# Memory attention's transposes and value products drawn together, and a delta-rule output moved, in a two-layer decoder trunk

## The chip, the cores and the metric

The kernel runs on one core of one Trainium2 chip. The metric is the device time of one execution in microseconds (us); the time before is the median of three runs.

## The reference, cut to what matters

Two layers over 256 tokens of 1024 channels. Each has a feed-forward block, then three token mixers in parallel on one normalised stream (a gated delta rule, a sliding-window attention, an attention over 256 memory rows), a gated merge, and a second feed-forward block. The change touches the memory attention and the order in which the delta rule's outputs are made:

```
def memory_cross_attention(q, mem_n, w_mem_kv):
    ...
    s = jnp.einsum('bshd,bmhd->bhsm', q, k).astype(jnp.float32) * (XA_DH ** -0.5)
    p = jax.nn.softmax(s, axis=-1)
    o = jnp.einsum('bhsm,bmhd->bshd', p.astype(v.dtype), v)
...
    def step(S, xs):
        q_i, qk_i, u_i, w_i, kt_i, gl_i = xs
        v_new = u_i - jnp.einsum('bhcd,bhde->bhce', w_i, S)
        o = jnp.einsum('bhcd,bhde->bhce', q_i, S) + jnp.einsum('bhcs,bhse->bhce', qk_i, v_new)
...
    gates = jax.nn.sigmoid(gates.reshape(B_, S_, N_BRANCH, D))
    merged = jnp.sum(gates * jnp.einsum('bsnc,ncd->bsnd', branches, w_branch), axis=2)
```

## The kernel before, in words

Weights come in one stream of units (128 x 1024 fp32) through SyncE's DMA queue into four `raw` buffers. ScalarE casts each to `whi` and VectorE forms the rest `wlo` (both at L123, five buffers each); TensorE then computes three fp32r products per tile (`mm3`), which is what the 128x512 rows named `acc` are. Small matrices of the mixers stay in plain fp32.

TensorE's order inside `mixers` is the order of the code (`pinned`). `weave(work, steps)` runs a generator of large projections and, after its n-th piece, the small steps that `steps` lists under n. `gates(n)` has eight pieces, one weight unit with 12 products of 128x512 each; `branch(n, o)` has four. The order is gates(0), branch(0), gates(1), branch(1), gates(2), branch(2), output projection. ScalarE, VectorE and the queues each run in an order that the scheduler fixes when the program is built.

The steps that matter here, for token blocks 0 and 1 (`tb` or `c`):

- `x_scores(tb)`: scores and softmax of the memory attention, into `prs[tb]` (tile `pp`, four ScalarE multiplies at L694 end it). `x_turn(tb)` (L698): 8 transposes into two accumulator banks, copied to `pt` by ScalarE and VectorE (L704). `x_values(tb)` (L706): 8 fp32 matmuls with the values into one bank (a timeline shows two passes for each fp32 matmul, so 16), split into `oX` by a cast and a subtraction (L123).
- The delta rule: `rec_s1` gives S1 (copied at L933). `rec_r1` multiplies it, and VectorE forms R1 from it head by head (L938, four instructions). `rec_v1` needs R1 and its result is copied at L945. `rec_qs` is read by VectorE at L942. `rec_o0` makes block 0's output from matrices that are long there; it is copied at L954, and `finish(0)` squares it (L912), sums (L913), takes an inverse root in small VectorE instructions and ends in two products (L918, L919). `rec_o1` does the same for block 1 (adding at L949). `finish_turn(c)` transposes the finished block for branch(2).

Accumulator banks come from three pools: `acc` four, `at` two, `sm` two. A step that draws a bank waits until the bank's last content has been read. All `rec_` steps, the products at L663 and `finish_turn` draw from `sm`; scores, `x_turn` and `x_values` from `at`.

Of the kernel before, what the change touches and what calls it, by code (L numbers as in the profile page):

```python
# [38 lines left out]
def tile_trunk(ctx, tc, x, xT, mem, memT_, wst, lnp, memln, cvw, rows, cst, out):  # L39
# [22 lines left out]
    def T(pool, shape, tag, dt=F32, bufs=None):  # L62
        pool = pn if pool is pu and tag in NEAR else pool
        kw = {} if bufs is None else {"bufs": bufs}
        return pool.tile(shape, dt, tag=tag, name=nm(tag), **kw)
# [4 lines left out]
    def at():  # L70
        return T(psT, [P, 512], "at")

    def sm():
        return T(psS, [P, 512], "sm")
# [47 lines left out]
    def split(hi, lo, src):  # L122
        return nc.scalar.copy(hi, src).ins, nc.vector.tensor_tensor(lo, src, hi.bitcast(F32), op=ALU.subtract).ins  # L123
# [7 lines left out]
    def matmul(*a, **k):  # L131
        return pe(nc.tensor.matmul(*a, **k))  # L132

    def transpose(*a):
        return pe(nc.tensor.transpose(*a))  # L135
# [7 lines left out]
    def weave(work, steps):  # L143

        for n, _ in enumerate(work, 1):
            for f in steps.get(n, ()):
                f()
# [369 lines left out]
    def mixers(l, hT, mkT, mv_, post):  # L517
# [141 lines left out]
        def products(c, hh):  # L659
            cc = slice(c * P, (c + 1) * P)  # L660
            ps = sm().rearrange("p (h a c) -> p h a c", h=2, a=2)
            for j in range(2):
                h = 2 * hh + j  # L663
                matmul(ps[:, j, 0, :], kT[:, h, cc], kT[:, h, cc], start=True, stop=True)
                matmul(ps[:, j, 1, :], kT[:, h, cc], qT[:, h, cc], start=True, stop=True)
            for j in range(2):
                h = 2 * hh + j
                nc.vector.scalar_tensor_tensor(AK[c][:, h], TM[c][:, 1][:, h, :].unsqueeze(1).to_broadcast([P, 2, P]), cS[:, c, h:h + 1], ps[:, j], op0=ALU.mult, op1=ALU.mult)
# [9 lines left out]
        def x_scores(tb):  # L678
            ts = slice(tb * P, (tb + 1) * P)
            pr = prs[tb] = T(p2, [P, 4, S], "pp")  # L680
            mxs = T(p3, [P, 4], "mx")
            sums = T(p3, [P, 4], "sums")
            for hh in range(2):
                ps = at().rearrange("p (h k) -> p h k", h=2)
                for j in range(2):
                    h = 2 * hh + j
                    mm3(ps[:, j, :], [t[:, h, ts] for t in xq], [t[:, h, :] for t in mkT], True, True)
                nc.vector.tensor_reduce(mxs[:, 2 * hh:2 * hh + 2], ps, axis=AX.X, op=ALU.max)
                nc.vector.tensor_scalar(mxs[:, 2 * hh:2 * hh + 2], mxs[:, 2 * hh:2 * hh + 2], -xs, None, ALU.mult)
                for j in range(2):  # L690
                    h = 2 * hh + j
                    nc.scalar.activation(pr[:, h, :], ps[:, j, :], AF.Exp, bias=mxs[:, h:h + 1], scale=xs, accum_out=sums[:, h:h + 1])
            nc.vector.reciprocal(sums, sums)
            [nc.scalar.mul(pr[:, h, :], pr[:, h, :], sums[:, h:h + 1]) for h in range(4)]  # L694
# [3 lines left out]
        def x_turn(tb):  # L698
            pT = prs[2 + tb] = T(p2, [P, 2, 4, P], "pt")
            for kb in range(2):  # L700
                ps = at().rearrange("p (h k) -> p h k", h=4)
                for h in range(4):
                    transpose(ps[:, h, :], prs[tb][:, h, kb * P:(kb + 1) * P], ident)
                (nc.vector.tensor_copy if kb else nc.scalar.copy)(pT[:, kb], ps)  # L704

        def x_values(tb):  # L706
            if not oX:
                oX.extend(T(pu, [P, 4, S], tag, F32R) for tag in ("u6", "u7"))
            ts = slice(tb * P, (tb + 1) * P)
            ps = at().rearrange("p (h k) -> p h k", h=4)  # L710
            for h in range(4):
                for kb in range(2):
                    matmul(ps[:, h, :], mv_[:, kb, h * P:(h + 1) * P], prs[2 + tb][:, kb, h, :], start=kb == 0, stop=kb == 1)
            split(oX[0][:, :, ts], oX[1][:, :, ts], ps)
# [245 lines left out]
        def gates(n):  # L960
            gt = gts[n] = [T(p2, [P, D], "gt") for _ in range(2)]
            for j in range(2):
                js = slice(j * 512, (j + 1) * 512)
                outs = [acc() for _ in range(2)]
                for uu in range(KD // 2):
                    hi, lo = unit()
                    for tb in range(2):
                        ts = slice(tb * P, (tb + 1) * P)
                        for kk in range(2):
                            k, c = 2 * uu + kk, slice(kk * 512, kk * 512 + 512)  # L970
                            mm3(outs[tb], (xt[0](k)[:, ts], xt[1](k)[:, ts]), (hi[:, c], lo[:, c]), k == 0, k == KD - 1)
                    if uu < KD // 2 - 1:
                        yield
                for tb in range(2):
                    nc.scalar.activation(gt[tb][:, js], outs[tb], AF.Tanh, scale=0.5)
                yield

        def branch(n, o):
# [16 lines left out]

        weave(gates(0), {
            1: [lambda: x_scores(1), lambda: products(1, 0), lambda: products(1, 1), inverses],
            3: [lambda: x_turn(0)],
            4: [lambda: x_values(0)],
            5: [lambda: x_turn(1)],  # L1000
            6: [lambda: x_values(1)],
            7: [lambda: w_scores(0, 0)],
            8: [lambda: w_scores(0, 1)]})
        weave(branch(0, oX), {
# [14 lines left out]
            3: [rec_s1],  # L1019
            4: [rec_r1]})  # L1020
        weave(gates(2), {
            1: [rec_o0],
            2: [rec_v1, rec_qs],
            3: [rec_o1],
            5: [lambda: finish_turn(0)],
            8: [lambda: finish_turn(1)]})
# [44 lines left out]
    ps = sm()  # L1071
# [15 lines left out]
    for l in range(NL):  # L1087
        mT = []
        mid = memory_T(mT, l)
        if l == 0:  # L1090

            more = {4: lambda *a: xres(0), 6: lambda *a: xres(1), 8: lambda *a: small()}
        post = Post(lnp[l, 0, 0], lnp[l, 0, 1])
        f1.rest(hT, 4, [((pu, "u0"), (pu, "u1")), ((pu, "u2"), (pu, "u3"))], post, mid, ends, {} if l else more)
        kv = memory_kv(mT, post.end)
        if l == 0:
            nc.scalar.activation(nea, rw[:, :, 8:12], AF.Exp)
            nc.vector.tensor_scalar(nea, nea, -1.0, None, ALU.mult)
        post2 = Post(lnp[l, 1, 0], lnp[l, 1, 1])
        mixers(l, post.hT, *kv, post2)  # L1100
        f2 = Ffn()
        begin(f2, post2.hT)
        last = l == NL - 1
        post = Post(lnp[l, 2, 0], lnp[l, 2, 1], last)
        f2.rest(post2.hT, 6, [((pu, a), (pu, b)) for a, b in (("u0", "u1"), ("u2", "u3"), ("u4", "u5"), ("u6", "u13"))], post, behind=post2.end)
        ends = post.end
        if not last:
            f1, hT = Ffn(), post.hT
            begin(f1, hT)
# [87 lines left out]
```

## Time and profile before

| | |
|---|---|
| median of 3 runs | 1274.8 us (1274.46 to 1275.08) |
| profiled execution, its own time | 1274.36 us |
| its span, first to last instruction | 1272.6 us |
| TensorE busy | 1260.9 us (99%) |
| VectorE busy | 865.0 us (68%) |
| ScalarE busy | 660.8 us (52%) |
| GpSimd busy | 206.9 us (16%) |
| mean granted clock of TensorE | 0.999 |

The profiled execution took 1.8 us more than its span, which is what lies around the first and the last instruction. In timelines a row is an instruction or a run of like ones: start, duration, engine, line, operation, tiles (out<-in), shapes, count, and in brackets the idle time of the engine before it with what ended it. Consecutive matmuls overlap in these rows, so what one costs is the distance between starts and not the duration shown.

### The profile page before, as it was taken

The page shows a single profiled execution, that of the slowest core. Times are in us where ns is not written, and L with a number is a line of the kernel's source. Part 1 is how long each engine was busy: PE and PEld are TensorE (multiplying, and loading weights), DVE is VectorE, ACT ScalarE, POOL GpSimd, SP SyncE. Part 2 cuts the span into 40 slices and gives each one's busy share as a digit, 9 for nine tenths or more (in the row PEclk, how much of TensorE's full clock was granted, in tenths as well). Part 3 has the DMA queues.
Part 4 walks back from the last instruction along what each step waited for, and adds up shares of the span by engine and source line. Part 5 has one row for each costly group of instructions (what it writes and reads, how often), then busy time and mean ns, then how long its engine had stood idle before and what let it go on. Part 6 is the DMA issues. An engine that isn't in the chain of part 4 may idle for free.

```text
span 1272.6 us, 18763 instructions
## 1 busy us (share of the span) xinstructions
PE 1260.9 (99%) x6948; PEld 1073.9 (84%) x6948; DVE 865.0 (68%) x1271; ACT 660.8 (52%) x980; POOL 206.9 (16%) x365
## 2 busy tenths in 40 slices
PE   9999999999999999999999999999999999999997
PEld 6888889999878888888888888899987788888886
DVE  5788576897657776665676665759867388666555
ACT  6556444655664544544454554456556564444541
POOL 0232100002311102221012220000024101122200
PEclk9999999999999999999999999999999999999999
DMA  8988755655534748777667877556453356577772
GB/s 296 305 274 280 254 209 164 206 166 142 171 118 138 245 135 264 240 242 221 218 208 242 255 254 215 182 184 213 152 168 133 100 185 229 172 247 244 241 231 73
DMA packets 77499, 261.40 MB, mean 205 GB/s; under 512 B 11904, under 2 KB 13056, under 8 KB 77408
## 3 DMA queue, kind: packets, MB, share of 16 engines
q1 hardware_dynamic: 66320, 232.53, 56.1%
q0 software_dynamic: 11088, 27.68, 7.8%
q8 instruction: 54, 0.88, 0.3%
q14 instruction: 37, 0.30, 0.1%
HBM read 246.40 MB, written 13.76 MB: 204 GB/s over the span
## 4 chain that ended last, share of the span: by engine, by line
PE 96%; DVE 2%; DMA 1%; ACT 1%; issue 0%; SPq 0%; DVEq 0%; ACTq 0%
PE acc L132 85%; PE at L132 4%; PE sm L132 3%; PE sm L135 2%; DVE wlo L123 1%; DMA raw<-in_wst_dram 1%; PE acc L326 1%; PE acc L327 1%; PE acc L329 1%; PE at L135 1%; ACT whi L123 1%; DVE h L289 0%; DVE pp L734 0%; DVE w L938 0%; SPq L115 0%
## 5 line engine op out<-in xcount | busy, mean ns | idle before, releaser
L123 DVE TENSOR_TENSOR wlo<-raw,whi 128x1024 fp32r<-128x1024 f32 (+2 forms) x403 | 488.8, 1220 | 284.9 <-ACT whi L123 282.8
L123 ACT CAST whi<-raw 128x1024 fp32r<-128x1024 f32 (+2 forms) x403 | 413.5, 1033 | 403.7 <-PE acc L132 322.0
L132 PE MATMUL acc<-whi,hT 128*128 128x512 f32 (+1 forms) x1824 | 562.7, 386 | 0.9 <-ACT whi L123 0.9
L132 PEld LDWEIGHTS acc<-whi,hT 128*128 128x128 f32 x1824 | 340.3, 188 | 70.1 <-ACT whi L123 2.5
L132 PE MATMUL acc<-wlo,hT 128*128 128x512 f32 (+1 forms) x912 | 350.3, 384 | 0.5 <-DVE wlo L123 0.5
L132 PE MATMUL acc<-whi,u 128*128 128x512 f32 x812 | 259.6, 392 | 0.0
L132 PEld LDWEIGHTS acc<-wlo,hT 128*128 128x128 f32 x912 | 171.4, 188 | 33.5 <-DVE wlo L123 1.2
L132 PEld LDWEIGHTS acc<-whi,u 128*128 128x128 f32 x812 | 152.3, 188 | 32.1 <-DVE u L123 0.5
L132 PE MATMUL acc<-wlo,u 128*128 128x512 f32 x406 | 158.2, 390 | 0.0
L356 POOL DMA_DIRECT2D tr<-t x176 | 96.3, 554 | 304.5 <-DVE t L350 296.4
L132 PE MATMUL acc<-hT,whi 128*128 128x256 f32 x672 | 122.2, 284 | 0.0
L132 PEld LDWEIGHTS acc<-hT,whi 128*128 128x128 f32 x672 | 104.6, 192 | 0.0
L132 PE MATMUL acc<-hT,wlo 128*128 128x256 f32 x336 | 95.0, 283 | 0.0
L132 PEld LDWEIGHTS acc<-wlo,u 128*128 128x128 f32 x406 | 76.3, 188 | 15.3
L132 PEld LDWEIGHTS acc<-hT,wlo 128*128 128x128 f32 x336 | 64.3, 192 | 0.0
L357 POOL DMA_DIRECT2D pt<-tr x44 | 25.0, 569 | 200.1 <-DMA tr<-t 129.1
L347 ACT ACTIVATE t<-acc 128x256 f32<-128x256 f32 x88 | 33.5, 380 | 37.1 <-PE acc L132 37.1
L132 PE MATMUL acc<-u,u 128*128 128x512 f32 x186 | 46.4, 394 | 0.0
L348 DVE TENSOR_TENSOR t<-t,acc 128x256 f32<-128x256 f32 x88 | 36.6, 416 | 8.6 <-ACT t L347 5.3
L993 POOL TENSOR_TENSOR u<-u,gt 128x512 f32<-128x512 f32 x16 | 20.7, 1295 | 124.9 <-DVE gt L991 124.9
L132 PEld LDWEIGHTS acc<-u,u 128*128 128x128 f32 x186 | 34.6, 188 | 7.5
L546 DVE SCALAR_TENSOR_TENSOR t<-acc,cw,t 128x255 f32<-128x255 f32 (+2 forms) x72 | 34.4, 478 | 1.0
(236 smaller groups left out, 1158.3 us busy)
## 6 DMA issues: line engine op xcount, KB each, us to landing
raw<-in_wst_dram SPq DMA_DIRECT2D x409, 512.0 KB, 4.4
tr<-t POOLq DMA_DIRECT2D x176, 64.0 KB, 3.9
pt<-tr POOLq DMA_DIRECT2D x44, 256.0 KB, 4.9
raw<-in_wst_dram SPq DMA_DIRECT2D x16, 324.0 KB, 3.0
gB<-in_lnp_dram SPq DMA_DIRECT2D x6, 512.0 KB, 5.4
bB<-in_lnp_dram SPq DMA_DIRECT2D x6, 512.0 KB, 6.2
w<-dr POOLq DMA_DIRECT2D x4, 512.0 KB, 11.0
t<-in_xT_dram SPq DMA_DIRECT2D x4, 256.0 KB, 5.4
```

What stands on the lines that cost most here:

```text
L123: return nc.scalar.copy(hi, src).ins, nc.vector.tensor_tensor(lo, src, hi.bitcast(F32), op=ALU.subtract).ins
L132: return pe(nc.tensor.matmul(*a, **k))
L135: return pe(nc.tensor.transpose(*a))
L326: nc.tensor.matmul(ps, hT[0][:, k, ts], hi[:, c], start=k == 0, stop=False)
L327: nc.tensor.matmul(ps, hT[0][:, k, ts], lo[:, c], start=False, stop=False)
L329: nc.tensor.matmul(ps, hT[1][:, k, ts], hi[:, c], start=False, stop=k == KD - 1)
L347: act = nc.scalar.activation(t[:, :, tb, :], g, AF.Silu).ins
L348: ins = nc.vector.tensor_tensor(t[:, :, tb, :], t[:, :, tb, :], u, op=ALU.mult).ins
L356: nc.gpsimd.dma_start(d[:, :, q].rearrange("b c x -> c b x"), z[32 * q:32 * q + 32].rearrange("c (b x) -> c b x", b=4))
L357: back = nc.gpsimd.dma_start(y, d.rearrange("b c q x -> (b c) (q x)")).ins
L546: nc.vector.scalar_tensor_tensor(yc[:, j, d:], b[:, j, :S - d], w[:, t:t + 1], yc[:, j, d:], op0=ALU.mult, op1=ALU.add)
L993: nc.gpsimd.tensor_tensor(mg[tb][:, js], mg[tb][:, js], gt[tb][:, js], op=ALU.add)
```

## The change: three groupings per layer

In gates(0), block 0's transposes move from piece 3 to piece 4 and block 1's from piece 5 to piece 4; block 0's value products move from piece 4 to piece 6, beside block 1's. Block 1's transposes draw their banks from `sm` and no longer from `at`. In gates(2), `rec_o0` moves from piece 1 to piece 2, behind `rec_v1` and `rec_qs`. No operation is added or removed.

```diff
         def x_turn(tb):
             pT = prs[2 + tb] = T(p2, [P, 2, 4, P], "pt")
             for kb in range(2):
-                ps = at().rearrange("p (h k) -> p h k", h=4)
+                ps = (sm if tb else at)().rearrange("p (h k) -> p h k", h=4)
                 for h in range(4):
                     transpose(ps[:, h, :], prs[tb][:, h, kb * P:(kb + 1) * P], ident)
...
         weave(gates(0), {
             1: [lambda: x_scores(1), lambda: products(1, 0), lambda: products(1, 1), inverses],
-            3: [lambda: x_turn(0)],
-            4: [lambda: x_values(0)],
-            5: [lambda: x_turn(1)],
-            6: [lambda: x_values(1)],
+            4: [lambda: x_turn(0), lambda: x_turn(1)],
+            6: [lambda: x_values(0), lambda: x_values(1)],
             7: [lambda: w_scores(0, 0)],
             8: [lambda: w_scores(0, 1)]})
...
         weave(gates(2), {
-            1: [rec_o0],
-            2: [rec_v1, rec_qs],
+            2: [rec_v1, rec_qs, rec_o0],
             3: [rec_o1],
             5: [lambda: finish_turn(0)],
             8: [lambda: finish_turn(1)]})
```

TensorE in gates(0) of the first layer, before (`cs` holds the identity, `pp` the probabilities, `pt` their transposes, `u_339` the values, `acc` rows belong to the gate projection):

```order
L132 MATMUL acc_2967<-whi_3104,hT_1598 128x512
L135 MATMUL at_3122<-cs,pp_2848 128x128 x4
L135 MATMUL at_3128<-cs,pp_2848 128x128 x4
L132 MATMUL acc_2966<-whi_3135,hT_1598 128x512
...
L132 MATMUL at_3156<-pt_3121,u_339_1830 128x128 x8
...
L135 MATMUL at_3188<-cs,pp_2986 128x128 x4
L135 MATMUL at_3194<-cs,pp_2986 128x128 x4
...
L132 MATMUL at_3218<-pt_3187,u_339_1830 128x128 x8
```

The same stretch of TensorE after the change:

```order
L132 MATMUL acc_2967<-whi_3122,hT_1598 128x512
L135 MATMUL at_3142<-cs,pp_2848 128x128 x4
L135 MATMUL at_3148<-cs,pp_2848 128x128 x4
L135 MATMUL sm_3155<-cs,pp_2986 128x128 x4
L135 MATMUL sm_3161<-cs,pp_2986 128x128 x4
L132 MATMUL acc_3167<-whi_3170,hT_1598 128x512
...
L132 MATMUL at_3207<-pt_3141,u_339_1830 128x128 x8
L132 MATMUL at_3218<-pt_3154,u_339_1830 128x128 x8
```

Four groups between projection pieces became two, and the second block's transposes fill `sm` banks.

TensorE in gates(2) of the first layer, before (`sm_3963` is `rec_o0`, `sm_4008` is `rec_v1`, `sm_4015` is `rec_qs`):

```order
L132 MATMUL acc_3943<-whi_3945,hT_1598 128x512
L132 MATMUL sm_3963<-w_461_2586,u_463_2588 128x128 x4
L132 MATMUL acc_3942<-whi_3991,hT_1598 128x512
...
L132 MATMUL sm_4008<-w_462_2587,w_471_2598 128x128 x4
L132 MATMUL sm_4015<-w_462_2587,u_386_2071 128x128 x4
```

The same stretch after the change, where `sm_3980` is `rec_v1`, `sm_3987` is `rec_qs` and `sm_3994` is `rec_o0`:

```order
L132 MATMUL acc_3943<-whi_3945,hT_1598 128x512
L132 MATMUL acc_3942<-whi_3963,hT_1598 128x512
...
L132 MATMUL sm_3980<-w_462_2587,w_471_2598 128x128 x4
L132 MATMUL sm_3987<-w_462_2587,u_386_2071 128x128 x4
L132 MATMUL sm_3994<-w_461_2586,u_463_2588 128x128 x4
```

`rec_o0` no longer stands ahead of a whole projection piece and of `rec_v1`, and three steps in a row now draw from the two `sm` banks.

VectorE around R1 (L938) in gates(2) after the change:

```order
L123 TENSOR_TENSOR wlo_4117<-raw_4115,whi_4116 128x1024
L938 SCALAR_TENSOR_TENSOR w_462_2587<-sm_3931,neg_460_2585,u_390_2075 128x128 x2
L123 TENSOR_TENSOR wlo_4135<-raw_4133,whi_4134 128x1024
L942 TENSOR_TENSOR t_697_3986<-sm_3987,eg_2584 128x512
L913 TENSOR_REDUCE oms_4001<-t_701_4000 128x4
...
L949 TENSOR_TENSOR t_697_3986<-t_697_3986,sm_4039 128x512
L123 TENSOR_TENSOR wlo_4153<-raw_4151,whi_4152 128x1024
...
L913 TENSOR_REDUCE oms_4046<-t_710_4045 128x4
L919 TENSOR_TENSOR t_705_4018<-t_705_4018,u_383_2058 128x512
```

Up to the last L938 the order is that of before; behind it block 0's finishing (L913 to L919), which came right after L938, now begins behind a weight split and L942 and has L949, a second split and block 1's L913 among its instructions.

## Rows read from the trace of the kernel before

**Rows 1.** The page: busy time of each engine, clock by slices, chain that ended last.

```profile
PE 1260.9 (99%) x6948; PEld 1073.9 (84%) x6948; DVE 865.0 (68%) x1271; ACT 660.8 (52%) x980; POOL 206.9 (16%) x365
...
PEclk9999999999999999999999999999999999999999
...
PE 96%; DVE 2%; DMA 1%; ACT 1%; issue 0%; SPq 0%; DVEq 0%; ACTq 0%
```

**Rows 2.** Waits of TensorE inside the mixers: total us, times, longest.

```profile
PE at L132 <- DVE pp L734: 0.4, 2, 0.2
PE sm L132 <- DVE w L938: 0.3, 2, 0.2
```

**Rows 3.** Timeline of TensorE, gates(0), first layer.

```profile
306.53 0.39 PE L132 MATMUL acc<-whi,hT 128*128 128x512 f32 x1
306.76 1.03 PE L135 MATMUL at<-cs,pp 128*128 128x128 f32 x8
...
307.86 0.39 PE L132 MATMUL acc<-wlo,hT 128*128 128x512 f32 x1
...
310.15 0.40 PE L132 MATMUL acc<-whi,hT 128*128 128x512 f32 x1
310.39 1.95 PE L132 MATMUL at<-pt,u 128*128 128x128 f32 x16
...
312.40 0.40 PE L132 MATMUL acc<-wlo,hT 128*128 128x512 f32 x1
...
323.06 0.40 PE L132 MATMUL at<-swk,u 128*128 128x256 f32 x2
```

**Rows 4.** Timeline of TensorE, gates(2), first layer, and one row of the second.

```profile
393.43 0.39 PE L132 MATMUL acc<-whi,hT 128*128 128x512 f32 x1
393.65 1.05 PE L132 MATMUL sm<-w,u 128*128 128x128 f32 x8
...
394.78 0.39 PE L132 MATMUL acc<-wlo,hT 128*128 128x512 f32 x1
...
397.07 0.39 PE L132 MATMUL acc<-whi,hT 128*128 128x512 f32 x1
397.62 1.13 PE L132 MATMUL sm<-w,w 128*128 128x128 f32 x8 [0.16 <-DVE w L938]
398.58 1.06 PE L132 MATMUL sm<-w,u 128*128 128x128 f32 x8
399.39 0.48 PE L132 MATMUL acc<-whi,hT 128*128 128x512 f32 x1
...
408.58 0.60 PE L135 MATMUL sm<-cs,t 128*128 128x128 f32 x4
...
1027.14 1.13 PE L132 MATMUL sm<-w,w 128*128 128x128 f32 x8 [0.15 <-DVE w L938]
```

**Rows 5.** Timeline of VectorE, gates(2), first layer.

```profile
395.12 1.83 DVE L123 TENSOR_TENSOR wlo<-raw,whi 128x1024 fp32r<-128x1024 f32 x1
396.88 0.59 DVE L938 SCALAR_TENSOR_TENSOR w<-sm,neg,u 128x128 f32<-128x128 f32 x2
397.39 0.67 DVE L913 TENSOR_REDUCE oms<-t 128x4 f32<-128x512 f32 x1
...
402.70 0.68 DVE L919 TENSOR_TENSOR t<-t,u 128x512 f32<-128x512 f32 x1
403.30 0.69 DVE L949 TENSOR_TENSOR t<-t,sm 128x512 f32<-128x512 f32 x1
```

**Rows 6.** Timeline of ScalarE, gates(0) and gates(2), first layer.

```profile
305.19 1.71 ACT L694 ACTIVATE pp<-pp,sums 128x256 f32<-128x256 f32 x4
...
394.04 1.05 ACT L123 CAST whi<-raw 128x1024 fp32r<-128x1024 f32 x1 [1.96 <-DMA raw<-in_wst_dram]
395.00 0.58 ACT L954 COPY t<-sm 128x512 f32<-128x512 f32 x1
395.61 0.64 ACT L912 ACTIVATE t<-t 128x512 f32<-128x512 f32 x1
...
398.78 0.59 ACT L945 COPY w<-sm 128x512 f32<-128x512 f32 x1 [0.24 <-PE sm L132]
```

## The prediction

> **What bounds the kernel now.** I read the page first. TensorE is busy 99% of the span, holds 96% of the chain that ended last, and its clock row is at the top in all forty slices [rows 1]. So a change is worth what it adds to or takes from TensorE's sequence, and only that: work moved elsewhere is free while it is in time. Then I read TensorE's waits. In the mixers there are two kinds, twice each (once a layer): 0.4 us for VectorE's L734 and 0.3 us for R1 at L938 [rows 2]. The whole mixer stage has 0.7 us of such idle time to win back, which already caps a gain from better cover. The second of these waits stands exactly where the change moves `rec_o0`, so the timelines of gates(2) decide the case.
>
> **What a group of small fp32 matmuls costs TensorE.** The change makes fewer, longer groups. If entering and leaving a group had a fixed price, three groups fewer per layer would be a gain. I measure from the last fp32r matmul ahead of a group to the second one behind it and take off two fp32r pitches. The pitch is 0.229: ten fp32r matmuls from 394.78 to 397.07 [rows 4]. Eight transposes: 307.86 - 306.53 - 0.46 = 0.87, or 0.109 each. One block's value products, eight fp32 matmuls that the trace shows as two passes each, sixteen in all: 312.40 - 310.15 - 0.46 = 1.79, or 0.112 a pass [rows 3]. `rec_o0`, eight passes: 394.78 - 393.43 - 0.46 = 0.89, or 0.111 each [rows 4]. A group twice as long costs twice as much, so no fixed part is left over; within the 0.01 us of these readings it is under 0.03 us a group. Six groups fewer in all: between 0 and -0.2 us. I take 0, because the pitch inside the long group equals the share of the short one.
>
> **gates(0), the transposes.** Block 0's 8 transposes come one piece later and block 1's one piece earlier. Block 1's probabilities are ready at 305.19 + 1.71 = 306.90 [rows 6]. TensorE reaches the new place at 310.39 - 0.87 = 309.52 and block 1's part 0.87 later [rows 3], more than 3 us after they are ready. The two `sm` banks were last used at piece 1, two units or more earlier. Cost 0. Their four copies have two pieces (2 x 12 x 0.229 = 5.5 us) before the value products need them; four copies of some 0.6 to 0.7 us on two engines fit. If that cover failed, the price would be the lateness, bounded by one copy behind one weight split (below 2 us a layer).
>
> **gates(0), the value products.** Now 3.58 us in one go, 2 x 1.79. They end where block 1's ended before, since the same work lies ahead. The `at` bank of block 0 is next wanted by the window scores at 323.06 [rows 3]. One piece (2.75 us) and the two products lie between, so block 0's products start near 323.06 - 2.75 - 3.58 = 316.7 and end near 318.5. A cast and a subtraction then have over 4 us. Cost 0.
>
> **gates(2), `rec_o0` as cover.** This is the term that counts. Before, TensorE issued its last projection matmul at 397.07 and could have begun `rec_v1` a pitch later at 397.30, but began at 397.62: 0.32 us lost on R1 [rows 4]. (The row shows 0.16 because the end of the matmul ahead is modelled.) R1's end is 396.88 + 0.59 = 397.47 [rows 5]. What sets it? The weight split at 395.12 stands ahead of R1's second half on VectorE [rows 5], that split waits for the cast at 394.04, and the cast for a weight DMA [rows 6]. The DMA was issued when an earlier split freed its buffer, behind ScalarE's copy of S1 in branch(1). Nothing in this line needs `rec_o0` or its copy, and the order of VectorE up to R1 is unchanged. So R1 is still ready at 397.47, and TensorE arrives 0.89 us earlier, at 396.41, without the work that had covered the wait. `rec_v1` starts at 397.62 as before; the 0.89 us become idle time. The second layer has the same wait, 0.15 in its row against 0.16 [rows 4], so it pays the same.
>
> **gates(2), `rec_o0` behind `rec_qs`.** It must wait for a bank: `rec_v1`'s, whose content ScalarE copies at 398.78 + 0.59 = 399.37 [rows 6]. The copy starts when TensorE delivers, so it keeps its time provided that ScalarE is free, and the 1.05 us cast that stands ahead of it waits for a projection piece that now ends 0.89 us earlier. TensorE finishes issuing `rec_qs` about 399.39 + 0.08 = 399.47 (eight pitches of 0.111 from 398.58). From copy to TensorE I take the 0.15 us from R1's end to `rec_v1`'s start, giving 399.52. The wait is 0 if the hand-over is quicker than that, 0.05 here, and at most 0.6 us if the copy comes late by its own length. I take 0.05. Then `rec_o0`'s 0.89 us run in the open.
>
> **What follows it.** `finish(0)` starts later. `rec_o0` now ends near 400.5; copy 0.58 and square 0.64 [rows 6] bring VectorE's sum to 401.8. Before, the way from L913 to the end of L919 was 403.38 - 397.39 = 5.99 us [rows 5]; less the split (1.23) and L942 (0.60) among it, its own work is some 4.2. Now L949 (0.69), a split (1.23) and block 1's L913 (0.67) lie among it: 401.8 + 4.2 + 2.6 = 408.6. `finish_turn(0)` wanted it at 408.58 [rows 4] and will want it 0.94 later, at 409.5. The slack shrinks from 5.2 us to 0.9 but holds. Cost 0, and the place to watch.
>
> **Sum.** Per layer 0.89 + 0.05 = 0.94; two layers 1.9 us. TensorE has no later wait that could absorb it. Against the profiled execution's own 1274.36 this gives 1276.3. That execution lies 0.4 below the median, 1274.8, of which the same sum gives 1276.7. I forecast the median: 1276.7, or +0.15%. About 0.2% (2.5 us) is what a measurement of this kernel can tell from no change.
>
> [...] After a group of eight transposes the next fp32r matmuls are at the full pitch, and the clock row shows the higher level throughout [rows 1, 3]. [...] No row here shows a group of sixteen transposes.
>
> **Rivals.**
> 1. *VectorE becomes the wait (slower).* At piece 5 of gates(2), block 0's L919 comes too late for `finish_turn(0)`. For: the slack falls to 0.9, and three foreign instructions stand in its chain, two of which depend on TensorE or ScalarE. Against: my chain has each at its measured length. It decides once the chain is more than 0.9 late. One further split (1.23) and one tile instruction (0.69) ahead make it 1.9 late, so 1.0 a layer: 1276.7 + 2.0 = 1278.7. Chance 0.15.
> 2. *R1 comes earlier too.* If R1's weight chain followed TensorE's earlier arrival, the 0.89 would not be idle time and only the bank wait stayed: about 1274.8 + 0.1 = 1274.9. Against: the row names a DMA, not TensorE, as what ended the cast's wait [rows 6]. Chance 0.07.
> 3. *Groups have a fixed price after all.* The first interval behind a group is 0.31 against 0.229 elsewhere; 0.08 x 6 = 0.5 us gained and no new stall: 1274.3. Against: group costs are proportional to their length. Chance 0.04.
> 4. [...] Chance 0.02.
>
> The order of instructions shows that all three groupings are in the program, so that the change does nothing is no rival.
>
> **How the numbers follow.** The forecast has 0.70, and 0.02 is left for what I have not seen. Its own range is 1275.9 to 1277.7: bank waits of 0 to 0.4 a layer, 0.2 for groups, 0.4 for the spread of runs. Outside it, 1274.9 and 1278.7 are the nearest rivals; the range 1274.8 to 1278.8 takes in both and leaves out the clock, the fixed price and chains that slip further. Slower by over 0.2% means above 1277.35: rivals 1 and 4 and a small end of the forecast, 0.20. Faster by over 0.2% would need 2.5 us where only 0.7 us of waits and 0.5 us of group edges exist: the 0.02 left over. The rest, 0.78, is within 0.2%.
>
> **What would show it.** In TensorE's waits, "sm <- DVE w L938" should grow from 0.3 to about 2.1 us, still twice, with `rec_v1` starting about 0.15 after L938 ends. A small wait of `rec_o0` for ScalarE's L945 may appear. Groups of 16 transposes should cost 1.75 and of 32 passes of value products 3.58. TensorE should enter piece 3 of gates(2) 0.9 to 1.0 later than before, counted from `rec_s1`. I am wrong if the L938 wait does not grow, if TensorE waits for `t` at L919, or if the stretch of gates(0) changes its length by more than 0.2 us.

## Result and profile after

The changed kernel takes 1278.47 us (median of 14 runs, 1277.38 to 1287.29), the kernel before beside it 1275.11 (median of 14, 1273.93 to 1279.21). The ratio is 1.0031, 95% interval 1.0021 to 1.0041: slower by 0.31%; by the medians 3.4 us. Ratios leave out the few executions that were disturbed, such as one of 1795.95 us at a granted clock of 0.655; medians keep them, which moves none by more than 0.3 us. The prediction was 1276.7. The measured time lies in its wide range (1274.8 to 1278.8) but outside the forecast's own (1275.9 to 1277.7), and the prediction had put 0.78 on a difference within 0.2%.

The profiled execution of the changed kernel took 1279.29 us with a span of 1277.3, 4.7 more than the span of before. Its page:

```profile
PE 1261.3 (99%) x6948; PEld 1074.3 (84%) x6948; DVE 863.4 (68%) x1271; ACT 659.7 (52%) x980; POOL 207.0 (16%) x365
...
PEclk9999999999999999999999999999999999999999
...
PE 93%; DMA 3%; DVE 2%; ACT 1%; issue 1%; SPq 0%; DVEq 0%; ACTq 0%
```

Against [rows 1] the work is the same and so is the clock. TensorE's busy time grew by 0.4 us. So the rest of the span is idle time of TensorE, and its waits must show it:

```profile
PE sm L132 <- DVE w L938: 2.2, 2, 1.1
...
PE sm L135 <- DVE h L290: 1.4, 1, 1.4
PE at L132 <- DVE pp L734: 1.2, 2, 1.0
```

Of the two waits of [rows 2], L938 grew from 0.3 to 2.2, as forecast (2.1). L734 grew from 0.4 to 1.2, which was not forecast. L290 is new: 1.4 us, at 636 us, outside the mixers. These are 1.9 + 0.8 + 1.4 = 4.1 of the 4.7 us. About 0.3 of the rest stands ahead of the changed places already: the products at the end of piece 1 of gates(0) start at 298.38 and not at 298.08.

TensorE's timeline in gates(0), which answers to [rows 3]:

```profile
309.55 0.39 PE L132 MATMUL acc<-whi,hT 128*128 128x512 f32 x1
309.78 1.03 PE L135 MATMUL at<-cs,pp 128*128 128x128 f32 x8
310.65 1.04 PE L135 MATMUL sm<-cs,pp 128*128 128x128 f32 x8
311.44 0.48 PE L132 MATMUL acc<-whi,hT 128*128 128x512 f32 x1
311.76 0.39 PE L132 MATMUL acc<-wlo,hT 128*128 128x512 f32 x1
...
316.77 0.40 PE L132 MATMUL acc<-whi,hT 128*128 128x512 f32 x1
317.00 3.73 PE L132 MATMUL at<-pt,u 128*128 128x128 f32 x32
320.49 0.48 PE L132 MATMUL acc<-whi,hT 128*128 128x512 f32 x1
320.81 0.40 PE L132 MATMUL acc<-wlo,hT 128*128 128x512 f32 x1
...
323.31 0.40 PE L132 MATMUL at<-swk,u 128*128 128x256 f32 x2
```

Inside gates(0) everything went as worked out. Sixteen transposes: 311.76 - 309.55 - 0.46 = 1.75. Thirty-two passes: 320.81 - 316.77 - 0.46 = 3.58. No wait stands in the stretch, and it ends 0.25 later than before (323.31 against 323.06), which is no more than the 0.3 with which it began. The cost comes 21 us later, at piece 1 of gates(1). VectorE there, after:

```profile
339.03 0.45 DVE L895 STREAM_TRANSPOSE w<-w 128x256 f32<-128x256 f32 x1 [4.94 <-POOL w L802]
339.40 4.59 DVE L123 TENSOR_TENSOR wlo<-raw,whi 128x1024 fp32r<-128x1024 f32 x4
343.91 1.28 DVE L734 SCALAR_TENSOR_TENSOR pp<-at,cs 128x512 f32<-128x512 f32 x2
```

and in the kernel before:

```profile
336.23 0.45 DVE L895 STREAM_TRANSPOSE w<-w 128x256 f32<-128x256 f32 x1 [2.40 <-POOL w L802]
338.24 4.63 DVE L123 TENSOR_TENSOR wlo<-raw,whi 128x1024 fp32r<-128x1024 f32 x4 [1.57 <-ACT whi L123]
342.79 1.28 DVE L734 SCALAR_TENSOR_TENSOR pp<-at,cs 128x512 f32<-128x512 f32 x2
```

L895 (in `begin_inverse`) waits for GpSimd's L802, which ends a chain of 30 GpSimd steps on the delta rule's inverse. Four weight splits and `w_scores(1,0)`'s L734 stand behind L895 on VectorE and do not need its result, but VectorE took them in order: the first split began 1.99 us behind the start of ScalarE's casts (337.41), where before it began 1.08 us behind it (337.16). Before, L895 was done 1.57 us before ScalarE's cast let the first split start: that was its slack. After, it starts 2.80 us later, uses the slack up, and L734 moves from 342.79 to 343.91. TensorE's `w_values` needs the `at` bank that L734 reads:

```profile
343.21 0.39 PE L132 MATMUL acc<-whi,hT 128*128 128x512 f32 x1
344.65 1.08 PE L132 MATMUL at<-pt,swv 128*64 128x512 f32 x4 [1.05 <-DVE pp L734]
```

Why GpSimd is late shows at its start. After:

```profile
311.82 1.23 POOL L788 DMA_DIRECT2D w<-dr  x2 [3.14 <-PE sm L135]
324.36 0.40 POOL L800 TENSOR_TENSOR t<-w,t 128x120 f32<-128x120 f32 x1 [11.31 <-issue]
```

and before:

```profile
311.61 1.24 POOL L788 DMA_DIRECT2D w<-dr  x2 [3.24 <-DMA dr<-t]
321.85 0.40 POOL L800 TENSOR_TENSOR t<-w,t 128x120 f32<-128x120 f32 x1 [9.01 <-issue]
```

L788 issues the two 512 KB loads that spread the inverse's blocks over the partitions. From their issue to L800 it took 12.54 us, before 10.24. The 2.3 us more, and 0.2 and 0.3 from the issue and the steps behind it, are L895's 2.8.

What ran beside them changed too. Of the weight loads (SyncE's queue, L115), three were issued in that time. After:

```profile
312.70 0.33 SPq L115 DMA_DIRECT2D raw<-in_wst_dram  x1
316.81 0.33 SPq L115 DMA_DIRECT2D raw<-in_wst_dram  x1
319.53 0.33 SPq L115 DMA_DIRECT2D raw<-in_wst_dram  x1
```

Before:

```profile
312.92 0.33 SPq L115 DMA_DIRECT2D raw<-in_wst_dram  x1
317.83 0.33 SPq L115 DMA_DIRECT2D raw<-in_wst_dram  x1
321.07 0.33 SPq L115 DMA_DIRECT2D raw<-in_wst_dram  x1
```

The second and third come 1.0 and 1.5 us earlier, because TensorE reaches projection pieces 4 to 6 earlier when the small work is put behind them, and so the weight buffers come free earlier: the casts that wait for these pieces start at 314.48 and 317.20 (before 315.11 and 318.74), and the splits behind them, for which the loads wait, end at 316.79 and 319.51 (before 317.80 and 321.05). From issue to landing these two took 9.3 and 7.9 us; before, 6.4 and 4.5. The first took 8.9, before 10.1. So the spreading loads and the last two weight loads lay over each other for longer, and these took longer.

In gates(2), which answers to [rows 4]:

```profile
397.25 0.39 PE L132 MATMUL acc<-whi,hT 128*128 128x512 f32 x1
398.73 1.13 PE L132 MATMUL sm<-w,w 128*128 128x128 f32 x8 [1.09 <-DVE w L938]
399.69 2.00 PE L132 MATMUL sm<-w,u 128*128 128x128 f32 x16
401.45 0.48 PE L132 MATMUL acc<-whi,hT 128*128 128x512 f32 x1
...
404.26 1.05 PE L132 MATMUL sm<-w,u 128*128 128x128 f32 x8
...
410.63 0.60 PE L135 MATMUL sm<-cs,t 128*128 128x128 f32 x4
...
1030.88 1.13 PE L132 MATMUL sm<-w,w 128*128 128x128 f32 x8 [1.08 <-DVE w L938]
```

`rec_v1` waits 1.09 and 1.08 us for R1 instead of 0.16 and 0.15: 0.93 more in each layer. Between `rec_qs` and `rec_o0` no wait is listed.

### The profile page after: what moved, and what is told of

Same layout as the page of the kernel before. It is cut to its first block, busy times and chain, and to the rows that moved or that the text cites. A ratio compares the mean times of both kernels' runs of the same rounds, so it can differ in the third digit from the quotient of the medians.

```text
span 1277.3 us, 18769 instructions
## 1 busy us (share of the span) xinstructions
PE 1261.3 (99%) x6948; PEld 1074.3 (84%) x6948; DVE 863.4 (68%) x1271; ACT 659.7 (52%) x980; POOL 207.0 (16%) x365
## 4 chain that ended last, share of the span: by engine, by line
PE 93%; DMA 3%; DVE 2%; ACT 1%; issue 1%; SPq 0%; DVEq 0%; ACTq 0%
PE acc L132 81%; PE at L132 4%; PE sm L132 3%; DMA raw<-in_wst_dram 2%; PE sm L135 2%; DVE wlo L123 1%; ACT whi L123 1%; PE acc L326 1%; PE acc L327 1%; PE acc L329 1%; PE at L135 1%; DMA bB<-in_lnp_dram 1%; DMA pt<-tr 0%; DVE h L290 0%; DVE h L289 0%
## 5 line engine op out<-in xcount | busy, mean ns | idle before, releaser
L132 PEld LDWEIGHTS acc<-wlo,u 128*128 128x128 f32 x406 | 76.3, 188 | 15.5
L123 DVE TENSOR_TENSOR u<-pt,u 128x512 fp32r<-128x512 f32 x44 | 28.9, 656 | 15.1 <-ACT u L123 15.1
## 6 DMA issues: line engine op xcount, KB each, us to landing
w<-dr POOLq DMA_DIRECT2D x4, 512.0 KB, 12.1
```

## Experiments

Two theories were set against each other for what goes beyond the forecast 1.9 us. By one (theory A in the expectations), gates(0) costs nothing, as forecast, and the rest is the spread of the runs. By the other (theory B), the regrouping in gates(0) costs too, through weight loads that come earlier, L788, GpSimd and L895. Edits are against the kernel before unless another is named. A ratio is to the kernel before, beside the run.

**The move of `rec_o0` alone.**

```diff
         weave(gates(2), {
-            1: [rec_o0],
-            2: [rec_v1, rec_qs],
+            2: [rec_v1, rec_qs, rec_o0],
```

> Only rec_o0 is moved behind rec_qs; gates(0) stays as before. Theory A (all that the change costs lies in gates(2)): TensorE's wait for L938 grows from 0.3 to about 2.2 us in total and the time by 1.9 us; what the changed kernel lost beyond that (some 1.5 us) was the spread of runs, so this kernel and the changed one take the same. Theory B (the grouping in gates(0) costs something too): 1.9 us over the kernel before, and 1 to 2 us less than the changed kernel. The wait of the window values for L734 stays near 0.2 a layer by both.

1277.02 us against 1275.28, ratio 1.0011 (1.0001 to 1.0022). L938 waits 2.2 us in all, L734 0.4 as before. By the medians 1.7 us of the 1.9 forecast: this term is right, and it is only about half of the result.

**The regrouping in gates(0) alone.**

```diff
-                ps = at().rearrange("p (h k) -> p h k", h=4)
+                ps = (sm if tb else at)().rearrange("p (h k) -> p h k", h=4)
...
-            3: [lambda: x_turn(0)],
-            4: [lambda: x_values(0)],
-            5: [lambda: x_turn(1)],
-            6: [lambda: x_values(1)],
+            4: [lambda: x_turn(0), lambda: x_turn(1)],
+            6: [lambda: x_values(0), lambda: x_values(1)],
```

> Only the memory attention is regrouped; rec_o0 stays in piece 1 of gates(2). Theory A: the time of the kernel before within 0.3 us, waits as before, 16 transposes at 1.75 and the value products at 3.58 us. Theory B: 1 to 2 us slower than before, with a wait of the window values for L734 that is over 0.2 us in at least one layer, because the load that spreads the inverse's blocks (L788) lands later.

1277.44 against 1275.28, ratio 1.0011 (1.0000 to 1.0022); by the medians 2.2 us. Its waits:

```profile
PE at L132 <- DVE pp L734: 1.7, 2, 1.6
...
PE sm L132 <- DVE w L938: 0.3, 2, 0.2
```

So the half of the change that was costed at nothing makes a wait of its own, at L734 and nowhere else in the mixers. This time it stands in the second layer (1.55) and not in the first. The interval touches 1, so the time alone would not have shown it; the waits do.

**`rec_o0` ahead of `rec_v1`, in the same piece.**

```diff
-            1: [rec_o0],
-            2: [rec_v1, rec_qs],
+            2: [rec_o0, rec_v1, rec_qs],
```

> rec_o0 in piece 2 of gates(2) but ahead of rec_v1; gates(0) as before. If rec_o0 is worth what it covers: R1's wait is 0.3 us in total as before, TensorE's time the same as before within 0.3 us, since the group of 24 passes costs what its parts cost. If the place of rec_o0 one piece later has a price of its own (its finish comes later by 2.7 us), it shows here as a wait at L919 or in the time.

1274.93, ratio 0.9996 (0.9987 to 1.0006). No wait for L938 is listed any more. Coming a piece later costs `rec_o0` nothing; standing behind the product that waits for R1 does.

**The change again.** The same kernel, beside the three above.

> The changed kernel a second time. Theory A: 2.0 us over the kernel before, and the two other waits of its first profile (1.0 us for L734 in the first layer, 1.4 us for L290 in the first layer's last normalisation) do not both come back. Theory B: 3 to 3.5 us over before, and the wait for L734 comes back near 1 us.

1279.12 (13 runs) against 1275.28, ratio 1.0019 (1.0008 to 1.0031); by the medians 3.8 us. No row of its profile is read, so what was expected of the waits was left to the further profiles below.

**The regrouping at earlier pieces.** As the regrouping alone, but the transposes at piece 3 and the value products at 4, so that all the small work lies behind pieces 3 and 4, where the change has it behind 4 and 6.

```diff
-            4: [lambda: x_turn(0), lambda: x_turn(1)],
-            6: [lambda: x_values(0), lambda: x_values(1)],
+            3: [lambda: x_turn(0), lambda: x_turn(1)],
+            4: [lambda: x_values(0), lambda: x_values(1)],
```

> Memory attention regrouped as in the change, but at pieces 3 and 4 of gates(0) where the change has 4 and 6; rec_o0 as before. TensorE then does the small work earlier and the projection later, so weight buffers come free no earlier than before. Theory B (the regrouping lets weight loads start up to 1.8 us earlier, into the load that spreads the inverse's blocks): no wait beyond 0.2 us for L734, time as before within 0.5 us. Rival (grouping as such costs TensorE or the other engines): 1.5 to 2 us slower, like the regrouping alone.

1274.68 against 1275.9, ratio 0.9991 (0.9982 to 1.0000). L734 waits 0.18 in both layers. The groups are as long as in the change and use the same banks, so neither length nor banks make a wait or cost time that shows. In this kernel the second weight load behind L788 is issued at 319.70, 8.4 us after it (before 6.2, change 5.0), and takes 5.4 us.

**The regrouping alone, with L895 behind L734.** `begin_inverse` moves from piece 3 to piece 4 of branch(0), behind `w_scores(1,0)`, and its transposes are issued after the last L734. Edit against the regrouping alone:

```diff
-                nc.vector.scalar_tensor_tensor(pr[:, 2 * j:2 * j + 2 * nj, :nk], ...
+                wpr["masked"] = nc.vector.scalar_tensor_tensor(pr[:, 2 * j:2 * j + 2 * nj, :nk], ...
...
-            with tc.issue_after(wpr["end"]):
+            with tc.issue_after(wpr["masked"]):
...
-            3: [lambda: w_turn(0, 1), begin_inverse],
-            4: [lambda: w_scores(1, 0)]})
+            3: [lambda: w_turn(0, 1)],
+            4: [lambda: w_scores(1, 0), begin_inverse]})
```

> Memory attention regrouped exactly as in the change, rec_o0 as before, and the VectorE instruction that waits for the inverse (L895) stands behind the window scores' L734 in place of ahead of four weight splits. Theory B (a late load reaches TensorE only through that wait at the head of VectorE's queue): the load may land as late as before or later, but L734's wait stays at 0.2 us a layer, and the time is that of the kernel before within 0.5 us. Rival (the loss is elsewhere in gates(0)): 1.5 to 2 us slower. Price of the move itself: TensorE's first doubling step may wait 0.1 to 0.2 us a layer for L895.

1275.16 against 1275.9, ratio 1.0000 (0.9990 to 1.0009). L734 waits 0.18 in the first layer, as expected, and 0.73 in the second, which was not; there L788 landed late again (up to 13.6 us after its issue). In its old place L895 would have waited for L802 there:

```profile
970.04 5.18 DVE L123 TENSOR_TENSOR wlo<-raw,whi 128x1024 fp32r<-128x1024 f32 x4 [4.31 <-ACT whi L123]
975.15 1.27 DVE L734 SCALAR_TENSOR_TENSOR pp<-at,cs 128x512 f32<-128x512 f32 x2
976.35 0.43 DVE L895 STREAM_TRANSPOSE w<-w 128x256 f32<-128x256 f32 x1
```

```profile
970.28 1.60 POOL L802 TENSOR_TENSOR w<-t,cs 128x256 f32<-128x256 f32 x1
```

L802 ends at 971.88, 1.8 us after the splits begin; in front of them, L895 would have held them that long. Behind them it holds nothing. What is left, 0.55 us over the usual 0.18, fits the four splits, which took 5.18 instead of some 4.6 us.

**The whole change, with L895 behind L734.** The edit just shown, on the changed kernel.

> The whole change with L895 behind L734. Theory B: what is left is the price of rec_o0, 1.9 us over the kernel before, with 2.2 us of waits for L938; faster than the change by 1 to 2 us. Rival: as slow as the change, 3.4 us over before.

1277.00 against 1275.9, ratio 1.0013 (1.0004 to 1.0022); by the medians 1.1 us, less than the 1.9 expected. L938 waits 1.08 in each layer, L734 0.18 and 0.72. Most of the part that was not forecast is gone; the part that was remains.

**The way forward.** The kernel before, with L895 behind L734 and `rec_qs` ahead of `rec_v1`, so that `rec_qs` covers R1 as well:

```diff
-            3: [lambda: w_turn(0, 1), begin_inverse],
-            4: [lambda: w_scores(1, 0)]})
+            3: [lambda: w_turn(0, 1)],
+            4: [lambda: w_scores(1, 0), begin_inverse]})
...
             1: [rec_o0],
-            2: [rec_v1, rec_qs],
+            2: [rec_qs, rec_v1],
```

> The kernel before with L895 behind L734 and with rec_qs ahead of rec_v1, so that 0.89 us of work that needs no R1 covers the wait for it. The L938 wait should vanish (0.3 us of idle time, 0.6 us of lost TensorE time in the two layers), and late inverse loads should cost nothing: 0.5 to 1.0 us faster than before, if the move of L895 costs no more than 0.1 us a layer.

1274.32 against 1275.9, ratio 0.9986 (0.9977 to 0.9996): faster than the kernel before by 0.14%, by the medians 1.6 us. In its trace no wait for L938 is listed, which explains 0.3 us. The rest was not taken apart, and the two moves were not tried one by one. The regrouping at earlier pieces, measured beside the same runs and expected to change nothing, also came out 1.2 us below by the medians; so how much of the 1.6 us belongs to the edit stays open.

**Four more profiles.** The wait at L734 came and went between layers, so the change was profiled twice more, the regrouping alone and the kernel before once more each.

> The change once more, for its profile. Theory B: the wait for L938 is 2.2 us as in the first profile; the wait for L734 is 0.2 in a layer where the load that spreads the inverse's blocks lands early and over 0.5 where it lands late, and the load takes 10 to 14 us. If the 1.4 us wait for L290 belongs to the change it comes back; if it is the spread of the weight loads it does not.

> A third profile of the change, with the same expectations: 2.2 us of waits for L938, L734 by the landing of the load, and L290 only by chance if it is the spread of the weight loads.

> The regrouping alone once more, for its profile. Theory B: no more than 0.3 us of waits for L938; in each layer the wait for L734 is what the landing of the load makes it, 0.2 us when early.

> The kernel before once more, for its profile. Theory B: weight loads at 6 and 9.5 us after the issue of the load that spreads the blocks, that load in 10 to 12 us, and a wait for L734 of 0.2 us in both layers.

They took 1278.68, 1276.40, 1277.71 and 1274.04 us. Here are all executions of which a trace is read and in which L895 stands in its old place. The second column is the time of L788's four loads of an execution, from issue to landing (minimum, median, maximum).

| execution | L788, us | waits for L734 by layer, us |
|---|---|---|
| before | 10.1, 11.0, 11.5 | 0.18, 0.18 |
| before, second profile | 10.8, 11.6, 12.1 | 0.17, 0.18 |
| `rec_o0` alone | 10.3, 11.2, 11.9 | 0.18, 0.18 |
| `rec_o0` first | 10.9, 11.5, 11.9 | 0.18, 0.18 |
| regrouped early | 10.3, 10.8, 11.2 | 0.18, 0.18 |
| change, first profile | 11.0, 12.1, 12.7 | 1.05, 0.18 |
| change, second | 11.7, 12.5, 13.0 | 0.35, 1.52 |
| change, third | 10.2, 11.4, 12.3 | 0.18, 0.18 |
| regrouping alone | 9.9, 12.3, 14.0 | 0.18, 1.55 |
| regrouping alone, second | 13.5, 14.0, 15.5 | 1.54, 1.57 |

Without the regrouping at pieces 4 and 6, ten layers of ten wait 0.17 or 0.18 us. With it, six of ten wait longer; the ten waits add up to 8.3 us, so 0.83 a layer, 0.65 more than before. That is 1.3 us an execution on average, between 0 and 2.8. The execution with a median of 11.4 at L788 has no extra wait, the one with 14.0 has it in both layers. With 1.9 for `rec_o0` this makes 3.2 us; the medians differ by 3.4.

The wait follows the end of GpSimd's chain. In the fourteen of these layers in which L802 starts at most 25.4 us after L788's issue, L734 waits 0.17 or 0.18; in the six in which it starts 25.7 us after it or later, 0.35 to 1.57. With L895 behind L734, an L802 that starts 26.6 and 26.7 us after L788 cost a wait of 0.73 and 0.72; in its old place, 26.7 to 26.9 cost 1.52 to 1.57.

The weight loads tell less. In all ten regrouped layers the second and third come equally early (4.8 to 5.0 and 7.5 to 7.7 us after L788; in the other ten not before 6.1 and 9.3), and yet four of them wait no longer than before. And the kernel of the way forward, not regrouped, has L802 at 25.7 and 25.8 us too. So early loads can at most make a late landing likelier.

## Why the prediction was wrong

**The step that failed** is "Cost 0" for gates(0), given twice, for the transposes and for the value products. What was examined there held: the probabilities, banks and copies were in time, and the stretch kept its length. But the prediction asked only what the moved work needs and who needs it. Moved small work also shifts the projection pieces around it, and with them the moment at which each weight buffer comes free and the next load is issued (here 1.0 and 1.5 us earlier). The prediction did not look at these loads or at GpSimd's queue in gates(0). The price came out as 1.3 us an execution, at a wait that [rows 2] had named (0.4 us for L734) and that the prediction did not follow back. With that term its sum would have been 1278.0, above the 1277.35 at which "slower by over 0.2%" begins; so the 0.78 on "within 0.2%" fell with it. Its own sign for being wrong, a change of length of gates(0) by over 0.2 us, could not have shown this cost, since TensorE pays it at piece 1 of gates(1).

That the price is paid because L895 stands ahead of L734 on VectorE is shown by the waits: they follow L802, and with L895 behind L734 a nearly equally late L802 costs less than half of the extra wait (0.54 and 0.55 us over the usual 0.18, against 1.34 to 1.39). The times agree, but their intervals overlap (1.0000 to 1.0022 for the regrouping alone, 0.9990 to 1.0009 with L895 moved). That earlier weight loads make L788 late is not shown. The early regrouping, in which the second and third loads come later than before and no landing is late, fits it, but no kernel changed the loads alone, and the landings also differ within one execution, by up to 4.1 us (9.9 to 14.0 in the regrouping alone).

**Right, point by point.** *Fixed price of a group*: none; 1.75 and 3.58 us were worked out and measured. *`rec_o0` as cover*: 0.93 a layer instead of 0.89; R1 later only by the 1.1 us by which this execution was late there; alone 1.7 us by the medians against 1.9. *Bank wait*: 0.05 was taken; none is listed, and `rec_qs` with `rec_o0` take 401.45 - 399.69 = 1.76 where 0.81 and 0.89 make 1.70, so 0.06. *`finish_turn(0)`*: the chain was to end at 408.6; by then this execution was 1.1 us later than before, which makes 409.7. VectorE's L919:

```profile
408.98 0.68 DVE L919 TENSOR_TENSOR t<-t,u 128x512 f32<-128x512 f32 x1
```

It ended at 409.66, and TensorE came to `finish_turn(0)` at 410.63. So the slack of 0.9 was right (0.97), and TensorE did not wait.

**Rivals.** VectorE as the wait at piece 5 gave almost the right time, 1278.7, for a reason that did not occur: no wait for L919 is listed. It had the right kind of mechanism, an engine that turns late with work queued behind the late instruction, at the wrong place. R1 earlier: no, 1.09 and 1.08 us of wait. A fixed price of groups: no. A fall of the clock, the 0.02 of rival 4: no trace shows one in long transposes, nor what it would cost; the sixteen transposes in gates(0) ran at 1.75 / 16 = 0.109 us each and the matmuls behind them at 0.23, the clock row stays in its top step, and the granted clock from 306 to 325 us is 1.00.

**Open.** The 1.4 us for L290 in the first profile of the change. VectorE waited there for a load of 512 KB of norm parameters:

```profile
635.54 1.42 DVE L290 SCALAR_TENSOR_TENSOR h<-h,rstd,bB 128x512 f32<-128x512 f32 x2 [2.35 <-DMA bB<-in_lnp_dram]
```

The same wait is 0.4 in the second profile of the regrouping alone and in the whole change with L895 behind L734, and is absent from the second and third profile of the change. It would account for the first profile being 4.7 us longer where the medians differ by only 3.4; whether the change makes it likelier was not tried.

## What to carry to other kernels

When small work moves among pieces that consume streamed weights, ask not only what the moved work needs: write down when each weight buffer comes free before and after, and which other transfers are in flight then. Then look on each engine for an instruction that waits for a far result and has urgent work queued behind it, as L895 had on VectorE; its slack (1.57 us here) is what any shift of transfers will use up. Cover for a late result must stand ahead of the first product that needs it in TensorE's order; that the work is in the same piece is not enough (2.2 us of waits for L938 with `rec_o0` behind `rec_v1`, none listed with it ahead).

## What the hardware showed that was not expected

Loads of one queue took much longer beside those of another: a weight load of 512 KB, 4.3 us in the median of the changed kernel, took 8.9, 9.3 and 7.9 us beside the two spreading loads of 512 KB each. Those took from 9.9 to 15.5 us in the traces of this case; what they take alone no run shows.

GpSimd and VectorE were slower side by side too: in the second layer of the regrouping alone and of the whole change, each with L895 behind L734, L802 took 1.60 us beside the weight splits, and the four splits took 5.18 and 5.17; with VectorE idle beside it, in the first layer of the kernel before and of the change, L802 took 0.74, and the four splits behind it 4.63 and 4.59.
